# A first norm moved ahead of its constants, a busy TensorE at entry, and five contraction-outermost groups in the first tile of an eight-core encoder kernel

## The chip, the cores and the metric

The kernel runs on all 8 cores of one Trainium2 chip. Each core computes one batch row of 4096 frames, and the cores do not communicate. The metric is the device time of the slowest core, in microseconds (us). The cores view of a profile counts cores 0 to 3 as die 0 and cores 4 to 7 as die 1.

Executions of this program come in two states: with the kernel before, five runs from 4569.86 to 4578.76 us and one of 5423.23 us. In the slow state the cores of one die, sometimes of both, show a lower granted TensorE clock and run some per cent longer (in the slow runs of the changed kernel 4763.0 to 5355.1 us at 0.838 to 0.949; the cores of its fast runs took 4558.4 to 4573.2 us at 0.995 to 0.998). Fast runs are compared with fast runs here. Where a profile fell into the slow state on one die, only its other die is read, and it is compared with the same die of the other kernel.

## The reference, cut to what matters

```python
for l in range(2):                                   # DEPTH
    h = rmsnorm(x, norm1_g[l])                       # x: (8, 4096, 1024) float32
    proj = einsum('bsd,de->bse', h, w_in[l])         # q,k,v,r,fz,B,C,x_in,g_A,g_B
    log_a = log_sigmoid(fz @ w_fg2[l] + b_fg[l]) / 16.0      # the forget gate
    o = gla_chunk_causal(q * 128**-0.5, k, v, log_a)         # chunks of 64 frames
    y_a = (headnorm(o) * gla_norm_g[l] * silu(r)) @ w_oa[l]
    y_b = (B * causal_conv3(C * x_in)) @ w_ob[l]
    x = x + (sigmoid(g_A) * y_a + sigmoid(g_B) * y_b) @ w_o[l]
    h2 = rmsnorm(x, norm2_g[l])
    x = x + (silu(h2 @ w_gate[l]) * (h2 @ w_up[l])) @ w_down[l]
return rmsnorm(x, final_g)
```

## The kernel before

A core does four phases (mixer, FFN, mixer, FFN), each over 8 tiles of 512 frames. The weights of a phase are streamed again for every tile, in blocks of mostly 1024 KB (bf16) through four slots of on-chip memory. The weights arrive in fp32. In the first tile of the first mixer the load itself casts them to bf16, and even blocks are stored to a bf16 scratch. The odd blocks are cast and stored in the second tile. From the third tile on, loads come from the scratch.

```python
if s == 0 or (s == 1 and bi % 2):                    # issue_loads: the cast loads
    dma("pool", [], [("ws", sl)], fsem[sl], ... in_=wblock(k, l, bi))
else:
    dma("sp", [("scr", k, l, bi)], [("ws", sl)], wsem[sl], ... in_=scr[(k, l, bi)])
...
if s == bi % 2 and steps[s][0] == 0:                 # get_block: store to the scratch
    dma("sp", [("ws", sl)], [("scr", k, l, bi)], stsem[sl], ...)
```

The kernel has eight banks of PSUM, `pb[0]` to `pb[7]`, and `bank()` gives them out in a ring, in program order. A mixer tile starts with the section below. With the ring reset at the tile's start, `fza` takes bank 0, q0 and q1 take 1 and 2, the gate's four products take 3 to 6, q2 and q3 take 7 and 0, and the four groups of the first v block take 1 to 4.

```python
def gate1():
    bs = [bank() for _ in range(4)]
    mms(...)                                         # four products of fza with wfg
    for hh in range(4):
        op("act", ... func=AF.Exp, scale=-1.0, ...)  # "the gate's first Exp" when hh == 0
        op("act", ... func=AF.Ln, bias=1.0)
...
sl, wk, w = get_block("fzq")
b = bank()
fm_group(b, w, wk, 0, h_, hk)                        # 8 matmuls
op("dve", [BK(b)], ["fza", BK(b)], ...tensor_copy(out=fza, in_=pb[b][:, :]))
for hh in range(4):
    if hh == 2:
        gate1()
    b = bank()
    fm_group(b, w, wk, 128 + hh * 128, h_, hk)
    op("act", [BK(b)], [("qT", hh), BK(b)], ...activation(out=qT[:, hh, :], in_=pb[b]...))
...
def v_half(hf, after):                               # v0 here, k, then v1
    sl, wk, w = get_block("v%d" % hf)
    for ts in range(NTS):
        b = bank()
        tm_group(b, w, wk, ts, h_, hk)
```

The entry of the program, before the first tile:

```python
load_x(0, "act")
issue_loads(1)
for n, t, src in (("cst", ...), ("pk", ...), ("wfg", ...)):
    dma("act", ...)
op("dve", ["cst"], ["ident16"], ...)                 # VectorE waits here for a DMA
...
op("dve", ["pk"], ["nbfg"], ...)
op("dve", [], ["ones32"], ...memset(ones32[:], 1.0 / D))
...                                                  # Pool waits for x, then:
issue_loads()
set_ring(list(range(8)))
norm_first()                                         # squares, sums on TensorE with ones32, h
```

## Time and profile before

The three timed runs took 4575.52, 4576.48 and 4578.76 us.

| what | number |
|---|---|
| TensorE busy, slowest core (1) | 99% of 4574.1 us |
| first Square on ScalarE | 9.31 us |
| first sum of squares on TensorE | 22.78 us |
| first h | 34.04 us |
| gate's first Exp, tiles one / two / three, mean of 8 cores | 44.3 / 215.2 / 387.9 us |
| spacing of that Exp in later mixer tiles, at full clock | 164.65 us |

The gate's first Exp serves as a milestone below: "gate two" is its time in the second tile. These are lines of the page of the kernel before. The first two are the span and the busy time of each engine; the third is the queue of cast loads (packets, MB, share of the 16 DMA engines' span); the last is the chain of waits by engine.

```profile
span 4574.1 us, 63583 instructions; the slowest of 8 cores (4548.1 to 4574.1 us)
PE 4520.0 (99%) x21880; PEld 2046.2 (45%) x21880; DVE 2014.2 (44%) x3171; ACT 1551.2 (34%) x2996; POOL 190.1 (4%) x348
...
q0 software_dynamic: 7392, 92.80, 15.1%
...
PE 95%; DMA 4%; DVE 0%; issue 0%; ACT 0%; ACTq 0%; SPq 0%; DVEq 0%; POOLq 0%
```

The kernel is bound by TensorE, except where weights arrive too slowly. 92.80 MB (counted in bf16) in 15.1% of 4574.1 us is 7.8 us of all 16 engines for a 1024 KB cast block.

The timeline of core 1's entry follows. A line has start, busy time, engine, source line, what was done, and in brackets the idle time or start of a wait and what ended it.

```profile
9.31 1.15 ACT L408 ACTIVATE sb_sq<-sb_xT 128x512 f32<-128x512 f32 x2
...
22.03 0.23 DVE L814 CAST sb_ident<-sb_cst 128x128 bf16<-128x128 f32 x1 [22.03 <-DMA sb_cst<-cst]
...
22.36 0.17 DVE L821 MEMSET sb_ones<- 128x128 f32 x1
22.78 9.59 PE L329 MATMUL pb<-sb_sq,sb_ones 128*128 128x512 f32 x16 [22.78 <-DVE sb_ones L821]
...
34.04 5.39 DVE L420 SCALAR_TENSOR_TENSOR sb_hT<-sb_xT,sb_pk,sb_rstd 128x512 bf16<-128x512 f32 x8 [4.31 <-ACT sb_rstd L400]
...
47.88 7.66 PE L329 MATMUL pb<-sb_wsl,sb_hT 128*128 128x512 bf16 x32
```

ScalarE had a square ready near 10.5 us. VectorE stood behind a constant's DMA until 22.03 us, so the `ones` for TensorE's sums came at 22.36 and all the sums after it.

The windows of core 1 show where the DMA engines are full. The columns are the window and its length; busy time and count of PE, PEld, DVE, ACT, POOL; the granted clock; the DMA share; GB/s.

```profile
60.00:110.00 50.00, 50.00 (x267) 22.93 (x266) 24.22 (x44) 24.55 (x52) 6.04 (x12) 1.00 1.01 191
160.00:210.00 50.00, 47.07 (x224) 20.87 (x222) 24.38 (x37) 4.50 (x12) 3.58 (x7) 1.00 1.01 210
280.00:400.00 120.00, 119.76 (x601) 54.23 (x600) 68.93 (x112) 51.29 (x110) 8.78 (x17) 1.00 0.77 222
```

In the first two tiles the DMA share is 1.01; later it is 0.77. TensorE idles 2.9 us (50 less 47.07) at the end of tile one. The wait table of core 1 from 36 to 4500 us (who waits for whom: total us, times, longest us) begins with the weight loads, and no wait for a q copy is in it:

```profile
PE pb L329 <- DMA sb_wsl<-w_mix: 6.0, 4, 4.4
```

Next, the start of the fourth tile on core 1, from the timeline. L494 is the gate's Exp, L532 the copies of q out of PSUM, and the matmuls with `sb_hT` on the right of `sb_wsl` are the v groups.

```profile
555.10 0.69 ACT L494 ACTIVATE sb_arena<-pb,sb_nbfg 128x512 f32<-128x512 f32 x1
...
557.09 7.07 PE L329 MATMUL pb<-sb_wsl,sb_hT 128*128 128x512 bf16 x32
...
560.53 1.07 ACT L532 ACTIVATE sb_arena<-pb 128x512 bf16<-128x512 f32 x2
```

The third q copy, the first of the pair at 560.53, ends at 561.11, after the third v group has started (560.54). It costs nothing before the change, because that v group uses another bank.

Three windows of the fourth tile on core 1 show a stretch at 0.81 of the full clock. The clock records of the trace give this level as 0.8125, or 13/16; the only other levels that they hold, on any core, are 1 and 0.5.

```profile
560.00:565.00 5.00, 5.00 (x24) 2.19 (x22) 4.69 (x8) 3.23 (x6) 0.00 (x0) 0.96 0.94 299
565.00:570.00 5.00, 5.00 (x20) 2.07 (x19) 2.37 (x4) 1.86 (x4) 0.00 (x0) 0.81 0.98 311
570.00:575.00 5.00, 5.00 (x23) 2.24 (x22) 1.38 (x2) 0.60 (x1) 0.00 (x0) 0.93 0.67 243
```

Such a stretch is called a dip below. Its loss is its length times 0.1875, which is 1 less 0.8125.

### The profile page before, as it was taken

How to read it: one execution, taken by the hardware profiler on the slowest of the kernel's cores; microseconds unless marked ns; L12 is line 12 of the kernel's file. 1: busy time of each engine (PE TensorE's matmuls, PEld its weight loads, DVE VectorE, ACT ScalarE, POOL GpSimd, SP SyncE). 2: the span in 40 equal slices, each digit the busy share in tenths (PEclk: the TensorE clock that was granted, in tenths of full speed). 3: DMA queues.
4: the chain of work that ended last, by engine and by line, in shares of the span. 5: the costliest groups of instructions: out<-in, count | busy, mean ns of one | idle time of the engine just before them, and what ended most of it. 6: DMA issues, size and time to landing. Idle time of an engine off the chain costs nothing.

```text
span 4574.1 us, 63583 instructions; the slowest of 8 cores (4548.1 to 4574.1 us)
## 1 busy us (share of the span) xinstructions
PE 4520.0 (99%) x21880; PEld 2046.2 (45%) x21880; DVE 2014.2 (44%) x3171; ACT 1551.2 (34%) x2996; POOL 190.1 (4%) x348
## 2 busy tenths in 40 slices
PE   7999999999999999999999999999999999999998
PEld 3444444444444444444444444444444444444443
DVE  3554555565562222222245655554554523333332
ACT  3453453344341111111143453353453322222221
POOL 0100000000000000000000000000000000000000
PEclk9999999999999999999999999999999999999999
DMA  9988777668778676676656565555555555555552
GB/s 199 211 228 237 198 178 209 188 168 213 201 180 240 200 211 197 196 206 197 189 170 194 152 202 187 171 176 190 171 168 195 187 188 189 189 185 187 189 189 88
DMA packets 124488, 870.23 MB, mean 190 GB/s; under 512 B 14512, under 2 KB 14640, under 8 KB 48048
## 3 DMA queue, kind: packets, MB, share of 16 engines
q1 hardware_dynamic: 115776, 770.75, 49.9%
q0 software_dynamic: 7392, 92.80, 15.1%
q8 instruction: 183, 3.00, 0.3%
q10 hardware_dynamic: 1008, 2.62, 0.2%
q14 instruction: 129, 1.06, 0.1%
HBM read 868.48 MB, written 148.37 MB: 222 GB/s over the span
## 4 chain that ended last, share of the span: by engine, by line
PE 95%; DMA 4%; DVE 0%; issue 0%; ACT 0%; ACTq 0%; SPq 0%; DVEq 0%; POOLq 0%
PE pb L329 90%; PE pb L341 4%; DMA sb_wsl<-w_mix 1%; DMA sb_xT<-xs 1%; PE pb L626 1%; DMA sc_mix_v<-sb_wsl 1%; DMA sc_mix_o<-sb_wsl 0%; DMA sb_cst<-cst 0%; DMA sc_mix_ob<-sb_wsl 0%; PE pb L515 0%; DMA sc_mix_oa<-sb_wsl 0%; DMA sb_wsl<-sc_mix_k 0%; DVE sb_hT L420 0%; DVE sb_xT L800 0%; ACTq L363 0%
## 5 line engine op out<-in xcount | busy, mean ns | idle before, releaser
L329 PE MATMUL pb<-sb_hT,sb_wsl 128*128 128x512 bf16 x8768 | 1948.6, 382 | 3.1 <-DVE sb_hT L420 1.9
L329 PEld LDWEIGHTS pb<-sb_hT,sb_wsl 128*128 128x128 bf16 x8768 | 851.1, 98 | 1065.7 <-issue 110.4
L329 PE MATMUL pb<-sb_arena,sb_wsl 128*128 128x512 bf16 x3324 | 729.0, 379 | 2.3 <-DMA sb_wsl<-w_mix 1.2
L329 PE MATMUL pb<-sb_hT,sb_arena 128*128 128x512 bf16 x3136 | 685.6, 380 | 2.0 <-ACT sb_tmp L761 2.0
L766 DVE TENSOR_TENSOR sb_arena<-pb,sb_tmp 128x512 bf16<-128x512 f32 x352 | 243.3, 691 | 779.8 <-PE pb L329 644.1
L761 ACT ACTIVATE sb_tmp<-pb 128x512 f32<-128x512 f32 x352 | 209.9, 597 | 1097.9 <-PE pb L329 1062.1
L329 PEld LDWEIGHTS pb<-sb_arena,sb_wsl 128*128 128x128 bf16 x3324 | 324.9, 98 | 396.5 <-issue 5.9
L329 PEld LDWEIGHTS pb<-sb_hT,sb_arena 128*128 128x128 bf16 x3136 | 307.5, 98 | 377.9 <-issue 14.7
L329 PE MATMUL pb<-sb_wsl,sb_hT 128*128 128x512 bf16 x2048 | 458.3, 381 | 4.4 <-DMA sb_wsl<-w_mix 4.4
L456 DVE TENSOR_TENSOR sb_xT<-pb,sb_xT 128x512 f32<-128x512 f32 x256 | 171.3, 689 | 615.5 <-PE pb L329 538.2
L329 PE MATMUL pb<-sb_arena 128*128 128x512 bf16 (+1 forms) x2052 | 388.3, 354 | 0.0
L329 PEld LDWEIGHTS pb<-sb_wsl,sb_hT 128*128 128x128 bf16 x2048 | 197.5, 98 | 242.9 <-issue 15.2
L329 PEld LDWEIGHTS pb<-sb_arena 128*128 128x128 bf16 (+1 forms) x2052 | 165.7, 97 | 208.6 <-issue 27.0
L532 ACT ACTIVATE sb_arena<-pb 128x512 bf16<-128x512 f32 x64 | 36.2, 591 | 589.4 <-PE pb L329 589.4
L668 DVE SCALAR_TENSOR_TENSOR sb_tmp<-sb_ub,sb_pk,sb_tmp 128x512 f32<-128x512 f32 x256 | 192.1, 750 | 79.6 <-ACT sb_halo L662 65.7
L341 PE MATMUL pb<-sb_arena,sb_wsl 128*128 128x512 bf16 x1024 | 226.2, 379 | 0.8 <-DVE sb_tmp L710 0.8
L438 DVE SCALAR_TENSOR_TENSOR sb_hT<-sb_xT,sb_pk,sb_rstd 128x512 bf16<-128x512 f32 x248 | 173.9, 746 | 30.8 <-ACT sb_rstd L400 26.4
L378 ACT ACTIVATE sb_sq<-sb_xT 128x1024 f32<-128x1024 f32 x152 | 159.4, 1049 | 43.4 <-DMA sb_xT<-xs 23.9
L661 ACT ACTIVATE sb_tmp<-sb_ub,sb_pk 128x512 f32<-128x512 f32 x128 | 103.9, 811 | 199.3 <-DVE sb_ub L658 197.1
L675 ACT ACTIVATE sb_arena<-pb 128x512 bf16<-128x512 f32 x256 | 149.8, 591 | 59.0 <-PE pb L329 55.8
L632 ACT ACTIVATE sb_arena<-pb,sb_pk 128x256 bf16<-128x256 bf16 x256 | 120.6, 471 | 140.1 <-PE pb L626 128.2
L587 DVE SCALAR_TENSOR_TENSOR sb_S_1<-sb_S_0,sb_gam,pb 128x256 f32<-128x256 f32 x256 | 122.5, 478 | 98.8 <-PE pb L329 83.0
(95 smaller groups left out, 2746.1 us busy)
## 6 DMA issues: line engine op xcount, KB each, us to landing
sb_wsl<-sc_mix_cv SPq DMA_DIRECT2D x116, 1280.0 KB, 7.7
sb_arena<-sc_ffn_f SPq DMA_DIRECT2D x98, 1024.0 KB, 5.8
sb_wsl<-sc_ffn_f SPq DMA_DIRECT2D x78, 1024.0 KB, 5.9
sb_arena<-sc_ffn_d SPq DMA_DIRECT2D x70, 704.0 KB, 5.2
xs<-sb_xT SPq DMA_DIRECT2D x48, 1024.0 KB, 6.0
sb_xT<-xs SPq DMA_DIRECT2D x96, 512.0 KB, 10.2
sb_wsl<-sc_ffn_d SPq DMA_DIRECT2D x58, 704.0 KB, 5.5
sb_wsl<-sc_mix_ob SPq DMA_DIRECT2D x30, 1024.0 KB, 5.7
```

Source lines behind the costliest of these rows:

```text
L329: return lambda pe: pe.matmul(out, lhsT, rhs, start=first, stop=last)
L341: ins = e.h.matmul(pb[b][:, :], w[:, kc, col0:col0 + 128], rhsT[:, kc, :], start=(kc == 0), stop=(kc == KC - 1))
L378: lambda h, j=j, i=i: h.activation(out=sq[i][:], in_=xT[xb][:, 2 * j:2 * j + 2, :], func=AF.Square))
L438: lambda h, kc=kc: h.scalar_tensor_tensor(out=hT[xb][:, kc, :], in0=xT[xb][:, kc, :], scalar=pkc(g0 + kc), in1=rstd[:], op0=ALU.mult, op1= ...
L456: lambda h, b=b, dc=dc: h.tensor_tensor(out=xT[xb][:, dc, :], in0=pb[b][:, :], in1=xT[xb][:, dc, :], op=ALU.add))
L587: lambda h, c=c, h2=h2, hh=hh: h.scalar_tensor_tensor(out=S32[1 - c][:, hh, :], in0=S32[c][:, hh, :], scalar=gam[:, hh, 2 * ts + c:2 * ts ...
L632: lambda h, src=src, dst=dst, par=par: h.activation(out=dst, in_=src, func=AF.Copy, scale=pkc(96 + l * 2 + par)))
L661: lambda h, u=u, cc=cc, cw=cw, cacc=cacc: h.activation(out=cacc[:], in_=ub[u][:, 2:T + 2], func=AF.Identity, scale=cw(2), bias=pkc(80 + l ...
L668: lambda h, j=j: h.scalar_tensor_tensor(out=cacc[:], in0=ub[u][:, j:T + j], scalar=cw(j), in1=cacc[:], op0=ALU.mult, op1=ALU.add))
L675: lambda h, b=b, dst=dst, cc=cc: h.activation(out=dst[:, cc, :], in_=pb[b][:, :], func=AF.Sigmoid))
L761: lambda h, b=b, si=si: h.activation(out=tmp[si][:], in_=pb[b][:, :], func=AF.Silu))
L766: lambda h, b=b, si=si, fc=fc: h.tensor_tensor(out=hid[:, fc, :], in0=pb[b][:, :], in1=tmp[si][:], op=ALU.mult))
```

## The change

The intent is to start TensorE's work earlier. VectorE writes `ones` first and does its constants after the norm. TensorE multiplies `ones` with itself while it waits. The aim is that the sums do not begin at half speed, as they did in the profile before (0.85 us a pass at first, 0.43 later); that this work would prevent it was the author's estimate. In the first tile the five q-section groups (`fza` and q0 to q3) go through the contraction together: all five use the first piece of h, then the second, and so on, so that they can start when the first piece is there. The code that arranges this takes five banks at once, and it does so in every tile. Cuts are marked with `...`.

```diff
         def norm_first():
-            b = bank()
+            b, b2 = bank(), bank()
+            def busy(n):
+                mms([BK(b2)], [(mm(pb[b2][:, 0:128], ones32[:, :], ones32[:, :], True, True), ["ones32"]) for _ in range(n)])
+            busy(40)
             for j in range(4):
 ...
                 for c in range(2):
                     mms(... sums of squares ...)
+                if j < 3:
+                    busy(6)
             tk.record([], [BK(b)], (tk.E["pe"].sem, tk.E["pe"].cnt, "pe"))
             rstd_of(b)
-            b = bank()
-            mms([BK(b)], [... for _ in range(12)])
+            busy(12)
 ...
             sl, wk, w = get_block("fzq")
-            b = bank()
-            fm_group(b, w, wk, 0, h_, hk)
-            op("dve", [BK(b)], ["fza", BK(b)], ...)
+            bs = [bank() for _ in range(5)]
+            if s == 0:
+                fm_groups_kco([(bs[i], w, wk, i * 128) for i in range(5)], h_, hk)
+            else:
+                fm_group(bs[0], w, wk, 0, h_, hk)
+            op("dve", [BK(bs[0])], ["fza", BK(bs[0])], ...)
             yield
             for hh in range(4):
                 if hh == 2:
                     gate1()
-                b = bank()
-                fm_group(b, w, wk, 128 + hh * 128, h_, hk)
+                b = bs[1 + hh]
+                if s:
+                    fm_group(b, w, wk, 128 + hh * 128, h_, hk)
                 op("act", [BK(b)], [("qT", hh), BK(b)], ...)
 ...
         issue_loads(1)
-        for n, t, src in (("cst", cst[:], cst_d), ("pk", pk[:], pk_d), ("wfg", wfg[:], wfg_d)):
-            dma("act", ...)
-        op("dve", ["cst"], ["ident16"], ...)
 ...
+        op("dve", [], ["ones32"], lambda h: h.memset(ones32[:], 1.0 / D))
 ...
-        op("dve", ["pk"], ["nbfg"], ...)
-        op("dve", [], ["ones32"], lambda h: h.memset(ones32[:], 1.0 / D))
+        for n, t, src in (("pk", pk[:], pk_d), ("wfg", wfg[:], wfg_d), ("cst", cst[:], cst_d)):
+            dma("act", ...)
 ...
         norm_first()
+        op("dve", ["pk"], ["nbfg"], ...)
+        op("dve", ["cst"], ["ident16"], ...)
```

With the change the q section takes banks 0 to 4 in every tile, the gate 5, 6, 7 and 0. The v groups still take 1 to 4, so the third v group must now wait until ScalarE has copied the third q group out of bank 3.

More of the change, by code (lines that the diff above doesn't have):

```diff
@@ L412, in norm_first @@
                     mms([BK(b)] if j + c == 0 else [], [(mm(pb[b][:, :], ones32[:, :], sq[i][:, c, :], j + c == 0, j + c == 4), ["ones32", ("sqh", i, c)])])
+                if j < 3:
+                    busy(6)
             tk.record([], [BK(b)], (tk.E["pe"].sem, tk.E["pe"].cnt, "pe"))
             rstd_of(b)
-            b = bank()
-            mms([BK(b)], [(mm(pb[b][:, 0:128], ones32[:, :], ones32[:, :], True, True), ["ones32"]) for _ in range(12)])
+            busy(12)
             for kc in range(KC):
@@ L521, in mixer @@
             sl, wk, w = get_block("fzq")
-            b = bank()
-            fm_group(b, w, wk, 0, h_, hk)
-            op("dve", [BK(b)], ["fza", BK(b)], lambda h, b=b: h.tensor_copy(out=fza, in_=pb[b][:, :]))
+            bs = [bank() for _ in range(5)]
[3 more added lines that the diff above has]
+                fm_group(bs[0], w, wk, 0, h_, hk)
+            op("dve", [BK(bs[0])], ["fza", BK(bs[0])], lambda h: h.tensor_copy(out=fza, in_=pb[bs[0]][:, :]))
             yield
@@ L809, in build_nc @@
         issue_loads(1)
-        for n, t, src in (("cst", cst[:], cst_d), ("pk", pk[:], pk_d),
-                          ("wfg", wfg[:], wfg_d)):
-            dma("act", [], [n], tk.newsem("c_" + n), lambda q, t=t, src=src: q.dma_start(out=t, in_=src))
-        op("dve", ["cst"], ["ident16"], lambda h: h.tensor_copy(out=ident16[:], in_=cst[:, 0:128]))
         epsb = sb("epsb", [128, 1], F32)
         lnp = sb("lnp", [128, 1], F32)
+        mhalf = sb("mhalf", [128, 4], F32)
+        op("dve", [], ["ones32"], lambda h: h.memset(ones32[:], 1.0 / D))
         op("dve", [], ["epsb"], lambda h: h.memset(epsb[:], EPS))
-        mhalf = sb("mhalf", [128, 4], F32)
         op("dve", [], ["mhalf"], lambda h: h.memset(mhalf[:], -0.5))
-        op("dve", ["pk"], ["nbfg"], lambda h: h.tensor_scalar_mul(out=nbfg[:], in0=pk[:, 108:116], scalar1=-1.0))
-        op("dve", [], ["ones32"], lambda h: h.memset(ones32[:], 1.0 / D))
+        for n, t, src in (("pk", pk[:], pk_d), ("wfg", wfg[:], wfg_d), ("cst", cst[:], cst_d)):
+            dma("act", [], [n], tk.newsem("c_" + n), lambda q, t=t, src=src: q.dma_start(out=t, in_=src))
         for q in xsem[0]:
@@ L826, in build_nc @@
         norm_first()
+        op("dve", ["pk"], ["nbfg"], lambda h: h.tensor_scalar_mul(out=nbfg[:], in0=pk[:, 108:116], scalar1=-1.0))
+        op("dve", ["cst"], ["ident16"], lambda h: h.tensor_copy(out=ident16[:], in_=cst[:, 0:128]))
         casts = {}
```

## The prediction

> **What bounds the kernel.** TensorE: the page gives it 99% busy, the chain of waits is 95% TensorE. From the third tile on a tile takes 165.4 us (spacing of the gate's first Exp in the timeline) and TensorE has no gaps (its waits after 400 us: 10 us in all, nearly all in the last norm). Two stretches differ. (1) Entry, slowest core: the first Square runs at 9.3 us, but VectorE's queue stands behind the constants (cast at 22.03 us, ones at 22.36), so all eight sums of squares run from 22.8 to 32.4, the first half at half speed (0.85 us a pass, later 0.43); Ln, Exp, then h from 34.04; the first matmul group is paced by h (0.66 us each) to 39.6. (2) Tiles one and two: in the windows the DMA share is 0.97 to 1.03 from 10 to 280 us. By the queue table the cast loads cost 92.8 MB in 15.1% of 16 engines' span, 7.8 us a 1024 KB block, 9.8 a 1280 KB one; with half the blocks stored, plus x, about 205 us of DMA time for tile one, against 168 us of TensorE work. TensorE starts with the loads 8 to 9 us ahead (landed 38.2, 45.7, 54.3; used 47.9, 54.8, 62.7), and at the tile's end waits for them (201 us; again 252 and 273).
>
> **What the change does at entry.** x still lands last at 21.1 us (third quarter 20.0). The squares start near 9 us; the 40 constant products (0.24 us each warm, double cold) keep TensorE going until about x's second half. After it: 2 sums, 6 fillers, 2 sums, about 5 us; Ln and Exp 1.4. First h at about 27 (before 34.0), first real matmul 28.4 (35.05), 40 matmuls at 0.216 end near 37 (the five groups and the gate ended at 48.9; now about 38.4). So TensorE is 8 to 10 us earlier at the first v block. [...]
>
> **What is left of it.** Loads after x are issued at 21.6 as before and DMA is saturated [...]. So TensorE meets the landings: waits at the conv blocks near 80 us and on, and the second tile starts nearly when it did (213.8 for its gate). I keep 1 to 2 us.
>
> **A cost in every later tile.** Five banks are now taken at once also for later tiles: third and fourth q groups move from banks 7, 0 to 3, 4; the third and fourth v groups use 3, 4 as before. Those q copies on ScalarE stand behind the gate's table load and eight Exp and Ln. In the timeline the third q copy ends 0.57 us AFTER the third v group starts, in every tile from the second on, on both cores read (395.90 against 395.34). Before, another bank hid it. Now TensorE waits 0.57 plus about 0.17 us for the release (read at the h pacing): 0.73 us in each of 14 TensorE-bound tiles, 10 us. In tile one the same wait is about 3 us, hidden by the loads.
>
> **Sum.** 4576.5 - 1.5 + 10.2 = 4585 us; range 4577 to 4589. Faster by over 2%: 0.003; within 2%: 0.99; slower: 0.007.
>
> **Shown right by:** first h near 27; TensorE waits on weight DMA growing by about 5 us before 280 us; gate of tile two within 3 us of 213.8; a new TensorE wait on ScalarE's q copy, 0.7 us, some 14 times; tile spacing 166.1 in place of 165.4.
>
> **Wrong if:** earlier issue makes loads land earlier, so up to 8 us stay (about 4578); the bank wait is hidden; or clock dips, about 1 us each, move.

The sum came to 4576.5 - 1.5 + 10.2 = 4585.2 us. That the constant products would keep the sums of x's second half at full speed is the author's estimate. Its figures are from the profile before: 24 passes on constants took 2.84 us from 32.21 us on, so a product of two passes took 0.24 us, and "double" is the ratio of the 0.85 and 0.43 us of the sums. The wait for DMA rests on the windows before, with a DMA share of 0.97 to 1.03 from 10 to 260 us.

## More of the kernel before

Experiments ran on several chips ("chip 6", "chip 14" and so on), and each has runs of the kernel before on that chip beside it.

Last, the granted clock. The cores view of the kernel before:

```profile
core 1: 4574.1 us, clock 0.993
...
die 0 (median of its cores): 4571.1 us, clock 0.993
die 1 (median of its cores): 4557.3 us, clock 0.997
```

Die 0 is 14 us slower than die 1, at a clock 0.004 lower.

Counting the trace's clock records, cores 0 to 3 had 21 or 22 dips each, worth 20.9 to 22.2 us; 14 or 15 of them began 7 to 14 us after a tile's gate. Cores 4 to 7 had none or one.

## The result and the profile after

The one fast run of the changed kernel among its six timed runs took 4573.28 us (two further executions, beside these six, were fast too: 4574.36 and 4572.33 us); the five fast runs of the kernel before took 4569.86 to 4578.76 us. Five runs of the changed kernel and one of the kernel before were in the slow state and are left aside. A ratio here is the mean time of one kernel's fast runs over that of the other's of the same rounds, so it is not quite the ratio of the medians quoted. The ratio of fast runs is 0.9995, with a 95% interval from 0.9977 to 1.0013: the same. The predicted class was right, but the predicted cost of 8.5 us did not appear, and 4573 lies below the range.

The profile of the changed kernel fell into the slow state on die 1, as its cores view shows:

```profile
core 1: 4567.5 us, clock 0.995
...
die 0 (median of its cores): 4570.4 us, clock 0.995
die 1 (median of its cores): 5315.0 us, clock 0.842
```

Die 0 is undisturbed and is compared with die 0 of before. This is core 1's entry after the change:

```profile
1.16 0.17 DVE L823 MEMSET sb_ones<- 128x128 f32 x1 [1.16 <-PEq L154]
1.48 10.67 PE L329 MATMUL pb<-sb_ones 128*128 128x128 f32 x80 [1.48 <-DVE sb_mhalf L825]
...
20.55 2.64 PE L329 MATMUL pb<-sb_sq,sb_ones 128*128 128x512 f32 x4 [2.29 <-ACT sb_sq L413]
...
28.96 5.39 DVE L425 SCALAR_TENSOR_TENSOR sb_hT<-sb_xT,sb_pk,sb_rstd 128x512 bf16<-128x512 f32 x8 [7.37 <-ACT sb_rstd L400]
29.99 8.79 PE L341 MATMUL pb<-sb_hT,sb_wsl 128*128 128x512 bf16 x40
...
40.21 3.61 PE L329 MATMUL pb<-sb_wsl,sb_hT 128*128 128x512 bf16 x16
...
46.44 3.61 PE L329 MATMUL pb<-sb_wsl,sb_hT 128*128 128x512 bf16 x16 [2.62 <-ACT sb_arena L541]
```

The first h comes 5.1 us earlier (28.96 against 34.04), and the first v group 7.7 us earlier (40.21 against 47.88). The third v group then waits 2.62 us for ScalarE's q copy (L541). By the second tile the lead is nearly gone: gate two moves from 216.3 to 214.9 us on core 1, and it is 1.3 to 2.4 us later on the three other cores of die 0.

These two windows of core 1 answer to those of before:

```profile
60.00:110.00 50.00, 47.03 (x250) 21.11 (x249) 24.37 (x43) 24.80 (x54) 6.01 (x12) 1.00 1.01 194
160.00:210.00 50.00, 48.57 (x229) 21.80 (x228) 25.05 (x38) 4.34 (x12) 3.58 (x7) 0.98 1.01 223
```

The DMA share is 1.01 as before, and TensorE now idles 3.0 us between 60 and 110 us, where it idled not at all. The longer of its two stops there ends like this:

```profile
81.84 0.32 SPq L299 DMA_DIRECT2D sc_mix_cv<-sb_wsl  x1
82.02 2.32 PE L329 MATMUL pb<-sb_hT,sb_wsl 128*128 128x512 bf16 x10 [1.74 <-DVE sb_arena L580]
```

The first line is the store of a conv block to the scratch, which is issued when the block has landed: at 81.78 us by the trace's semaphore record, against 80.97 before. The next conv block landed at 102.57 us, against 102.47 before. So the loads are no earlier, but TensorE is: before, it came to the first of these blocks only at 85.55. The view names VectorE for this wait and ScalarE for the other (1.16 us), but both stopped matmuls are the first of a block and start 0.24 to 0.25 us after its landing, as the one at 251.30 does, for which the table names a DMA. An earlier issue did not help either: the first block of r weights was issued at 39.33 us instead of 48.58 but landed at 65.40 instead of 62.65. The last block of tile one landed at 200.05 instead of 201.30.

The start of the fourth tile on core 1 shows the predicted bank wait:

```profile
554.89 0.69 ACT L499 ACTIVATE sb_arena<-pb,sb_nbfg 128x512 f32<-128x512 f32 x1
...
556.88 3.62 PE L329 MATMUL pb<-sb_wsl,sb_hT 128*128 128x512 bf16 x16
...
560.33 1.07 ACT L541 ACTIVATE sb_arena<-pb 128x512 bf16<-128x512 f32 x2
561.05 3.18 PE L329 MATMUL pb<-sb_wsl,sb_hT 128*128 128x512 bf16 x14 [0.55 <-ACT sb_arena L541]
```

Counted from the gate's first Exp, the third v group starts 0.72 us later than before (6.16 us after it, against 5.44); 0.55 us of this is shown as idle time. The wait table of core 1, from 30 us on, counts the wait 16 times, the first of them (2.6 us) in tile one:

```profile
PE pb L329 <- ACT sb_arena L541: 11.1, 16, 2.6
PE pb L329 <- DMA sb_wsl<-w_mix: 6.0, 3, 4.3
```

At full clock a tile is now 165.36 us long, 0.71 us more than the 164.65 of before. The same three windows of that tile, though, have lost their dip:

```profile
560.00:565.00 5.00, 4.45 (x22) 1.86 (x21) 4.06 (x7) 3.03 (x6) 0.00 (x0) 1.00 1.01 366
565.00:570.00 5.00, 5.00 (x25) 2.29 (x24) 2.85 (x5) 1.87 (x4) 0.00 (x0) 1.00 0.99 338
570.00:575.00 5.00, 5.00 (x27) 2.29 (x25) 1.38 (x2) 0.60 (x1) 0.00 (x0) 1.00 0.54 168
```

On die 0, no dip begins near a gate any more; 9 or 10 a core remain elsewhere in the program. The means over cores 0 to 3 add up as follows:

| die 0, mean of 4 cores | before | after | difference |
|---|---|---|---|
| start to gate three | 387.4 us | 389.0 us | +1.6 |
| gate three to end | 4183.0 us | 4181.2 us | -1.8 |
| of it: 14 bank waits of 0.71 us | | | +9.9 |
| of it: lost in dips after gate three | 18.37 us | 6.46 us | -11.9 |

The last two rows sum to -2.0 us, against -1.8 measured. So the wait was there in the predicted size, and fewer dips paid for it. This is one profile of each kernel; that the bank order and not chance took the dips away is tested below.

### The profile page after: what moved, and what is told of

Same layout as the page of the kernel before. It is cut to its first block, busy times and chain, and to the rows that moved or that the text cites. A ratio compares the mean times of both kernels' runs of the same rounds, so it can differ in the third digit from the quotient of the medians.

```text
span 5327.9 us, 63749 instructions; the slowest of 8 cores (4567.5 to 5327.9 us)
## 1 busy us (share of the span) xinstructions
PE 5292.3 (99%) x21996; PEld 2239.1 (42%) x21996; DVE 2023.3 (38%) x3171; ACT 1561.7 (29%) x2996; POOL 187.5 (4%) x348
## 3 DMA queue, kind: packets, MB, share of 16 engines
q1 hardware_dynamic: 115776, 770.75, 41.8%
q10 hardware_dynamic: 1008, 2.62, 0.2%
## 4 chain that ended last, share of the span: by engine, by line
PE 95%; DMA 4%; ACT 0%; issue 0%; DVE 0%; ACTq 0%; POOL 0%; POOLq 0%; SPq 0%; DVEq 0%
PE pb L329 89%; PE pb L341 5%; DMA sb_wsl<-w_mix 2%; DMA sc_mix_cv<-sb_wsl 1%; PE pb L635 1%; DMA sc_mix_k<-sb_wsl 0%; DMA sb_xT<-x 0%; DMA sc_mix_o<-sb_wsl 0%; DMA sc_mix_ob<-sb_wsl 0%; PE pb L520 0%; DMA sb_wsl<-sc_mix_k 0%; ACT sb_arena L499 0%; ACT sb_arena L502 0%; DVE sb_xT L809 0%; ACT L499 0%
## 5 line engine op out<-in xcount | busy, mean ns | idle before, releaser
L329 PE MATMUL pb<-sb_hT,sb_wsl 128*128 128x512 bf16 x8728 | 2239.9, 424 | 5.3 <-DMA sb_wsl<-w_mix 4.7
L329 PEld LDWEIGHTS pb<-sb_hT,sb_wsl 128*128 128x128 bf16 x8728 | 915.6, 106 | 1292.0 <-issue 1075.7
L329 PE MATMUL pb<-sb_arena,sb_wsl 128*128 128x512 bf16 x3324 | 854.9, 425 | 0.2 <-DMA sb_wsl<-w_mix 0.2
L329 PE MATMUL pb<-sb_hT,sb_arena 128*128 128x512 bf16 x3136 | 829.7, 436 | 0.0
L770 ACT ACTIVATE sb_tmp<-pb 128x512 f32<-128x512 f32 x352 | 210.2, 597 | 1432.0 <-PE pb L329 1386.6
L329 PEld LDWEIGHTS pb<-sb_arena,sb_wsl 128*128 128x128 bf16 x3324 | 354.5, 107 | 489.9 <-issue 414.6
L329 PEld LDWEIGHTS pb<-sb_hT,sb_arena 128*128 128x128 bf16 x3136 | 341.1, 109 | 486.4 <-issue 486.4
L329 PE MATMUL pb<-sb_wsl,sb_hT 128*128 128x512 bf16 x2048 | 524.1, 419 | 10.1 <-DMA sb_wsl<-w_mix 5.1
L329 PE MATMUL pb<-sb_arena 128*128 128x512 bf16 (+1 forms) x2052 | 463.0, 401 | 0.0
L329 PEld LDWEIGHTS pb<-sb_arena 128*128 128x128 bf16 (+1 forms) x2052 | 182.2, 105 | 265.7 <-issue 263.8
L341 PE MATMUL pb<-sb_arena,sb_wsl 128*128 128x512 bf16 x1024 | 259.4, 418 | 0.6 <-DMA sb_wsl<-w_mix 0.6
L541 ACT ACTIVATE sb_arena<-pb 128x512 bf16<-128x512 f32 x64 | 36.1, 591 | 674.4 <-PE pb L329 665.0
L667 DVE TENSOR_TENSOR sb_ub<-pb,sb_tmp 128x512 f32<-128x512 f32 x128 | 88.5, 691 | 242.0 <-PE pb L329 230.3
L341 PEld LDWEIGHTS pb<-sb_arena,sb_wsl 128*128 128x128 bf16 x1024 | 107.2, 105 | 142.2 <-issue 105.9
```

Source lines behind the costliest of these rows:

```text
L329: return lambda pe: pe.matmul(out, lhsT, rhs, start=first, stop=last)
L341: ins = e.h.matmul(pb[b][:, :], w[:, kc, col0:col0 + 128], rhsT[:, kc, :], start=(kc == 0), stop=(kc == KC - 1))
L667: lambda h, b=b, u=u, csb=csb: h.tensor_tensor(out=ub[u][:, 2:T + 2], in0=pb[b][:, :], in1=csb[:], op=ALU.mult))
L770: lambda h, b=b, si=si: h.activation(out=tmp[si][:], in_=pb[b][:, :], func=AF.Silu))
```

## The experiments

There were 18 runs. Three questions were asked: does the bank change alone make both the wait and the missing dips; is the entry's gain lost to the DMA engines; and is the short pause of TensorE itself what removes the dips? The theory was "yes" to each. The rivals were chance or a property of the chip for the dips, and, for the entry, a gain taken by the bank wait of tile one.

### Parts of the change, on chip 6

`e1_banks_only` is the kernel before with the five banks taken at once, in the order of computation of before.

```diff
             sl, wk, w = get_block("fzq")
-            b = bank()
-            fm_group(b, w, wk, 0, h_, hk)
+            bs = [bank() for _ in range(5)]
+            fm_group(bs[0], w, wk, 0, h_, hk)
 ...
-                b = bank()
+                b = bs[1 + hh]
```

> The kernel before, with only the five banks of the q section taken at once in every tile. Theory (loads absorb the entry's gain; the bank wait costs 0.7 us a tile; its pause also removes the 13/16 clock dips that stand in the same place, 1.1 us each): a wait of TensorE on the q copy about 15 times, 0.7 us each; undipped cores 165.36 us a tile in place of 164.65; on a die that dipped before, the dips 8 to 13 us after the gate gone, so the slowest core is within 3 us of before. Rival (the entry's gain of 8 to 10 us reaches the end and pays for the bank wait; the dips come and go by chance): 10 us slower than before, and dips where they were.

`e2_banks_back` is the changed kernel with five banks at once in the first tile only, the order of before in the others.

```diff
-            bs = [bank() for _ in range(5)]
+            bs = [bank() for _ in range(5 if s == 0 else 1)]
 ...
-                b = bs[1 + hh]
+                b = bs[1 + hh] if s == 0 else bank()
```

> The changed kernel with the old order of banks in every tile but the first. Theory: no wait on the q copy after tile one, undipped cores back at 164.65 us a tile, the dips after the gate back on the die that has them, the whole within 3 us of before. Rival: about 10 us faster than before and than the changed kernel, 4564 to 4567 us.

`e3_entry_only` is the changed kernel with the whole q section of before, in every tile: only the norm and the constants are changed.

```diff
-            bs = [bank() for _ in range(5)]
-            if s == 0:
-                fm_groups_kco([(bs[i], w, wk, i * 128) for i in range(5)], h_, hk)
-            else:
-                fm_group(bs[0], w, wk, 0, h_, hk)
+            b = bank()
+            fm_group(b, w, wk, 0, h_, hk)
 ...
-                b = bs[1 + hh]
-                if s:
-                    fm_group(b, w, wk, 128 + hh * 128, h_, hk)
+                b = bank()
+                fm_group(b, w, wk, 128 + hh * 128, h_, hk)
```

> The constants and the fillers of the entry alone, no contraction outermost, banks as before. Theory: first h near 29 us in place of 34, and the gate of the second tile within 2 us of before (213 to 217 us), whole within 2 us of before. Rival: gate of the second tile and the end 5 us earlier.

`e4_changed_again` is the changed kernel, unedited.

> The changed kernel once more, for a profile with both dies undisturbed. Theory: undipped cores 165.36 us a tile, gate of the second tile 213 to 217 us, few dips after the gate; whole within 3 us of before.

On this chip the kernel before ran at 4603.5 to 4630.8 us (median 4616.0 of 11 runs), slower than on the chip of the first result. Its dips are longer, 15.1 us each in e3's profile, and hit die 1 (the kernel before was not traced on this chip). A die that dips enough is over 1% longer than the other, so some of these runs are labelled slow; the ratios use only those labelled fast. `e1` gave 0.9949 [0.9899, 0.9998], `e4` 0.9946 [0.9894, 0.9998], `e2` 0.9997 [0.9894, 1.0100]; `e3` got no interval, and its fast runs took 4618.65 and 4613.81 us. Within the 2% class all are the same. `e1` and `e4` were expected within 3 us of before and came out about 24 us faster by these ratios: dips cost more on this chip than on the first, from which the expectation was made.

The reason is plainer core by core. The next table takes all runs of this chip, slow ones too, and picks cores instead of runs: in the middle column the cores whose mean granted clock was at least 0.996, and at the right cores 4 to 7 wherever their clock was above 0.97, which leaves out the slow state. In brackets is the number of cores averaged.

| chip 6 | cores at full clock | cores 4 to 7, dipping |
|---|---|---|
| before | 4553.3 us (40) | 4604.4 us (44) |
| e3: entry only | 4554.1 (25) | 4597.9 (28) |
| e2: all but the banks of later tiles | 4553.2 (11) | 4596.1 (32) |
| e1: banks only | 4564.0 (24) | 4579.9 (16) |
| e4: the change | 4564.7 (29) | 4580.2 (24) |

At full clock the banks cost 10.7 us (e1) and the entry is worth nothing (e3 and e2 within 1 us of before). On cores 4 to 7 the banks alone gain 24.5 us. The slowest core is a dipping one, so the time follows the right column. Single runs scatter: the means of these four cores in a run reach from 4568 to 4605 us with the new bank order (e1 and e4) and from 4576 to 4611 us with the old one (before, e2, e3), but six of the ten runs with the new order lie below all 26 with the old. Two fast-state profiles show it. First a line of the cores view and three windows of e3, core 4:

```profile
core 4: 4617.5 us, clock 0.982
```

```profile
565.00:570.00 5.00, 5.00 (x21) 2.13 (x20) 3.21 (x5) 1.86 (x4) 0.00 (x0) 0.84 0.97 279
570.00:575.00 5.00, 5.00 (x20) 2.07 (x19) 2.02 (x3) 0.00 (x0) 0.00 (x0) 0.81 0.95 334
575.00:580.00 5.00, 5.00 (x26) 2.38 (x25) 0.75 (x2) 1.59 (x2) 0.00 (x0) 0.81 0.67 248
```

Then the same of e4, core 4:

```profile
core 4: 4587.8 us, clock 0.991
```

```profile
560.00:565.00 5.00, 4.46 (x22) 1.86 (x21) 3.27 (x5) 4.71 (x9) 0.00 (x0) 1.00 0.82 299
565.00:570.00 5.00, 5.00 (x25) 2.28 (x24) 4.07 (x7) 2.47 (x6) 0.00 (x0) 1.00 1.00 336
570.00:575.00 5.00, 5.00 (x25) 2.29 (x24) 2.00 (x3) 0.06 (x1) 0.00 (x0) 1.00 0.70 206
```

In the clock records of these profiles, cores 4 and 5 of e3 had 26 dips each (73.7 us lost), 15 of them near a gate. In e4, cores 4 to 7 had 10 each (28.4 us lost), none near a gate. In e1, cores 4 and 5 had 9 each (25.5 us lost) and one near a gate. The profile of e2 was slow on die 0; on its other die, 13 to 15 dips a core began near a gate. So the dips near the gate go with the bank order: they are there in before (on the first chip), e2 and e3, and all but gone in e1 and e4. The difference in dips from e3 to e4 (-45.3 us) and the waits (+10) would make core 4 faster by 35 us; it is faster by 29.7, and the rest was not traced.

The traces of e1 to e4 that are kept are of other executions, with other core times. What remains of the first profiles agrees in size with the counts: the views above, and the mean clock of core 4 (0.982 in e3, 0.991 in e4). In the kept traces, e1, e2 and e3 have at most two dips a core and none near a gate, and e4 has a few long stretches, so they say nothing for or against the link. They do confirm the price of the bank order at full clock: 164.66 us a tile in e2 and e3, 165.36 in e1 and e4.

### The pause alone, and a later entry, on chip 14

`e5_pause_only` keeps the banks and the entry of before but makes the third v group wait for the third q copy, which is the wait that the bank order causes.

```diff
-                    tm_group(b, w, wk, ts, h_, hk)
+                    tm_group(b, w, wk, ts, h_, (lambda kc: hk(kc) + [("qT", 2)]) if (ts, hf) == (2, 0) else hk)
```

> The kernel before with its own banks, but the third v group of each tile made to wait for the third q copy, which it does not need. If the pause of TensorE is what removes the clock dips: a wait of 0.7 us in each tile from the second on, undipped cores 165.36 us a tile, no dips 8 to 14 us after the gate, and a time within 0.3% of the kernel with the banks alone (0.995 of before on a chip that dips much, 1.00 on one that dips little). If it is the change of banks and not the pause: 165.36 us a tile and the dips still there, 10 us slower than before.

`e6_pause_short` does the same with an earlier event, the gate's last Ln, for a shorter pause.

```diff
-                    tm_group(b, w, wk, ts, h_, hk)
+                    tm_group(b, w, wk, ts, h_, (lambda kc: hk(kc) + [("spb", 3)]) if (ts, hf) == (2, 0) else hk)
```

> The same, but waiting for the gate's last Ln, which ends 0.08 us after the group would start: a pause of about 0.25 us. If any break in the dense stretch does: 164.9 us a tile on undipped cores, no dips after the gate, 7 us less than with the long pause. If the break must be long: the dips stay, and the time is before's plus 3 us.

`e7_late` is the changed kernel with 40 more constant products ahead of the first h's matmuls.

```diff
-            busy(12)
+            busy(52)
```

> The changed kernel with 52 in place of 12 fillers after the norm, so that the first real matmul comes 9.5 us later (39.5 us in place of 30). If the loads of tile one absorb the entry's gain: gate of the second tile at most 3 us later than in the changed kernel (213 to 221 us). If the gain reaches the end: 9.5 us later (223 to 227 us).

The kernel before ran at full clock on this chip, on all 60 cores of its undisturbed dies (a mean granted clock of 0.996 or more leaves no room for the dips of chip 6, where 73.7 us of 4617.5 were lost, 0.016 of the clock), and its fast runs took 4559.27 to 4563.51 us. So the question about the pause could not be answered here. What was measured is the price. Averaged over full-clock cores, before takes 4556.0 us, e5 4566.6 (+10.6), e6 4560.1 (+4.1). The tile spacing grew by 0.71 us in e5 and by 0.22 us in e6. The ratios are 1.0024 [0.9995, 1.0054] and 1.0024 [0.9984, 1.0064]. A fast run of e5 at 4599.94 us had a long stretch of low clock on each core of die 1 (261 us from 28 us on for cores 4 and 5, 106 to 124 us from 4461 us on for cores 6 and 7). None of them began near a gate.

In e7 the gate of tile one came at 48.6 us on average over the cores, against 39.9 in e4, yet gate two came at 218.4 us, against 216.2. The products that made it late stand in the timeline of core 1:

```profile
28.12 11.77 PE L329 MATMUL pb<-sb_ones 128*128 128x128 f32 x104
39.73 2.54 PE L341 MATMUL pb<-sb_hT,sb_wsl 128*128 128x512 bf16 x11
```

An entry 8.7 us later than in e4 made gate two only 2.2 us later. Tile one, from gate to gate, took 169.8 us instead of 176.3: most of the delay was absorbed, as it is if the loads set the tile's end.

### DMA relieved in tile one, and stores spread out, on chip 4

`e8_before_nostore` and `e9_changed_nostore` are the kernel before and the changed kernel with no stores in tile one: all blocks are cast again in tile two and stored then.

```diff
-                if s == 0 or (s == 1 and bi % 2):
+                if s == 0 or s == 1:
 ...
-            if s == bi % 2 and steps[s][0] == 0:
+            if s == 1 and steps[s][0] == 0:
```

> The kernel before, with all stores of bf16 weight blocks moved from the first tile to the second (about 35 us of DMA time less in tile one, more in tile two). Serves as the base of the next run. If loads bound tile one: the gate of the second tile a few us earlier than in before (208 to 213 us), TensorE without waits on weights in tile one; the third tile later.

(The 35 us are an estimate. On the profile page of before, the queue that carries the stores (q1) moved 770.75 MB in 49.9% of the span, 3.1 us of all 16 engines for 1024 KB, and the ten blocks stored in tile one hold 11520 KB.)

> The changed kernel with the same move. If the first tile's DMA load is what absorbed the entry's gain, the gate of the second tile now comes 5 to 8 us earlier than in the run before it (202 to 207 us). If something else absorbs it: no more than 2 us earlier.

All three runs of e8 were slow. In e9 the TensorE of core 4 waits for no DMA at all in tile one. The first line of its wait table from 36 to 212 us (the only other is 0.2 us for VectorE), and a window with the DMA share at 0.79:

```profile
PE pb L329 <- ACT sb_arena L541: 2.8, 1, 2.8
```

```profile
110.00:160.00 50.00, 50.00 (x266) 22.88 (x265) 34.22 (x57) 33.06 (x73) 8.24 (x13) 1.00 0.79 129
```

`e10_spread` is e2 with the stores spread over the first four tiles by a fixed list, and the casts of the next phase begun one tile later (the last edit is not shown).

```diff
+        STORE_AT = [0, 1, 2, 3, 1, 0, 2, 1, 0, 3, 2, 1, 0, 2, 3, 0, 1, 2, 0, 3]
 ...
-                if s == 0 or (s == 1 and bi % 2):
+                if p_of(s) == 0 and s <= STORE_AT[bi]:
 ...
-            if s == bi % 2 and steps[s][0] == 0:
+            if steps[s][0] == 0 and s == STORE_AT[bi]:
```

> The changed kernel with the old banks after tile one and the stores spread over tiles one to four (6, 5, 5, 4 blocks), the first casts of the next weights one tile later. If the loads of tiles one and two cost about 15 us beyond TensorE's work and hid the entry's gain of 8 us: the gate of the third tile 10 to 20 us earlier than before's 388, and the whole 10 to 20 us under before on cores without dips; dips as before's.

`e11_spread_short` is e10 with the short pause of e6.

> The same with the short pause (third v group waits for the gate's last Ln). If the short pause removes the dips after the gate as the long one did: no dips 8 to 14 us after the gate on dies that show them in the run before it, and faster than it there; on dies without dips 0.22 us a tile slower, 3 us in all. If it is too short: dips in both runs alike.

In e10 gate two came at 206.1 us, about 9 us earlier than before, but gate three at 391.2, later than before (387.9). The wait table of core 5 from 30 to 400 us says where it went:

```profile
PE pb L332 <- DMA sb_wsl<-sc_mix_r: 15.0, 1, 15.0
```

One block of tile two was issued at 212.49 us and landed at 252.10. The gain of tile one was given back in one wait of tile two. Fast runs took 4577.62 and 4585.17 us against 4562.27 to 4565.74 for before. All runs of e11 were disturbed (lowest 4617.91), so it decides nothing.

### Another spread, the pauses again, on chip 12

`e12_spread2` has e10's edits with another list: it stores the first six blocks in tile one and the others one to three tiles later, and fetches the next tile's x later in the first two tiles. The casts of the next phase begin as in e10.

```diff
+        STORE_AT = [0, 0, 0, 0, 0, 0, 1, 2, 3, 1, 2, 3, 1, 2, 3, 1, 2, 3, 1, 2]
 ...
-                side += [lead(8), pre(), lead(8 if kind == "ffn" else 34), norm_h(s + 1)]
+                side += [lead(26 if s < 2 else 8), pre(), lead(8 if kind == "ffn" else 16 if s < 2 else 34), norm_h(s + 1)]
```

> The changed kernel with old banks after tile one, the six blocks that a tile needs first stored in tile one (so tile two starts on short loads), the other 14 in tiles two to four, and x of tiles two and three fetched 18 groups later. If the e10 kernel's wait at the start of the second tile (12 to 16 us on the second r block, loads of 25 to 40 us) came from casts, x and stores piled up there: that wait under 4 us, gate of the third tile at 370 to 380 us (before 388), and on cores without dips 10 to 18 us under before. If the loads cannot be evened out: gate of the third tile at 385 or later, no gain.

`e13_pause_again` is e5 and `e14_short_again` is e6, unedited, tried on another chip. `e15_before_nostore` repeats e8.

> The pause without the change of banks once more, for a chip whose kernel before shows dips (the first try fell on one without). If the pause removes the dips: none 8 to 14 us after the gate, faster than before by 0.7 us a tile less than the dips' loss. If the banks did it: the dips there, 10 us slower than before. On a chip without dips: 10 us slower either way.

> The 0.25 us pause once more. Dips after the gate gone if any break will do; still there if the break must be longer. Without dips on the chip: 3 us slower than before.

> The kernel before with the stores of tile one moved to tile two, once more, for a profile in the fast state: the base of the changed kernel with the same move, whose second gate came at 210 us. If loads absorbed the entry's gain: gate of the second tile 4 to 6 us later than there (214 to 217), the first tile 165 to 166.5 us long from gate to gate in both, in place of 171 and 176 with the stores.

The kernel before again ran at full clock, on all 48 cores of its undisturbed dies (4554.6 us on average). e13 took 4564.1 us on such cores (+9.5), e14 4557.3 (+2.7; ratio 1.0007 [0.9978, 1.0036]), e12 4558.6 (+4.0; ratio 1.0017 [0.9988, 1.0046]). No spread of the stores made the program faster. e12 missed its expected gate three of 370 to 380 us: in its profile, which was slow on die 1, the four cores of die 0 reached it at 381.6 to 394.7 us. By the wait table of core 0, no wait for a DMA before 400 us was longer than 1.7 us; what held gate three back was not traced.

Chip 12 is not quite free of dips near the gate. One run of before had die 0 at a clock of 0.985, as on chip 6, and was not traced. In e12, which has the old bank order after tile one, cores 2 and 3 had five dips near the gates of later tiles; in e13 and e14, with the pauses, no core had one in a later tile. But e15, without a pause, had only one such dip on each of four cores, so these profiles don't decide it.

e15 completes the test of the entry. In both no-store kernels tile one is bound by TensorE (165.9 us from gate to gate in e15, 165.6 in e9), and core 4's waits in tile one of e15 hold no DMA either:

```profile
PE pb L329 <- DVE sb_hT L420: 1.3, 5, 0.3
```

| mean of 8 cores | gate one | gate two | gate three |
|---|---|---|---|
| before (first chip) | 44.3 us | 215.2 us | 387.9 us |
| the change, e4 (chip 6) | 39.9 | 216.2 | 388.9 |
| e15: before, no stores in tile one (chip 12) | 49.5 | 215.3 | 427.6 |
| e9: the change, no stores in tile one (chip 4) | 44.7 | 210.2 | 426.6 |

(The e4 row is from its first profile; die 0 of the profile after gives 39.6, 215.8 and 389.0 us.)

Without stores in tile one, the change's lead is 4.8 us at gate one and 5.1 us at gate two: it passes through, although e9 has the wait for the q copy in tile one too (2.8 us). With them, 4.4 us at gate one becomes -1.0 at gate two. Both no-store kernels then pay over 45 us in tile two, where all blocks are cast again, and there the lead shrinks to 1.0 us: DMA is the bound there too (core 4 of e9 waits 43 us for weights between 212 and 430 us). (Gate one is about 5 us later in both no-store kernels than in the kernels with stores, so e9 is compared with e15, not with before.) The two ran on different chips and there is one profile of each; no core of either lost more than 3 us to dips in the whole run.

### A last try of the pause, on chip 4 again

`e16_before_look` is the kernel before, `e17_pause_third` is e5 and `e18_short_third` is e6, all unedited.

> The kernel before, for its profile on this chip: tells whether the chip shows dips 8 to 14 us after the gate (as the first chip and chip 6 did) or none (chips 14, 4, 12), and so what the two runs after it can tell.

> Pause of 0.7 us, old banks. If the profile of the run before it shows dips after the gate: none here if the pause removes them, the same number if the banks did. Without dips there: 165.36 us a tile and 10 us slower.

> Pause of 0.25 us, old banks. With dips on this chip: gone if any break will do, there if it must be longer. Without: 164.88 us a tile and 3 us slower.

e16 ran at full clock (4559.22 us), and its trace has no dip on any core. Its gates came at 44.1, 214.4 and 387.6 us, and its later mixer tiles are 164.65 us long on all cores. On full-clock cores before takes 4552.7 us, e17 4562.3 (+9.6) and e18 4557.1 (+4.4; ratio 1.0039 [0.9991, 1.0088]). Before, e17 and e18 each also had runs in which two or four cores were some 30 to 50 us longer at a clock of 0.984 to 0.991, with the pause and without it; where it was traced (e17, e18), it was one stretch of 161 us on a pair of cores, not a row of dips. So no try of the pause alone met a kernel before that was seen to dip at the gate on the same chip: the traces of e16 show none here, and on chips 14 and 12 the kernel before was not traced.

## Why the prediction was right and wrong

**The entry came earlier: right, less than predicted.** The first h was predicted near 27 us and came at 28.96 us; the five groups were predicted to end near 37 us and ended at 38.78 (29.99 plus 8.79). TensorE idled 2.29 us before the sums of x's second half, and the clock records show a stretch at half clock of 3.4 us at 22 us, so part of those sums ran at half speed in spite of the constant products (2.64 us for four passes, which take 0.43 us each at full clock). What sets off such a stretch was not shown.

**The lead is absorbed: right.** Gate two was predicted within 3 us of 213.8; on die 0 it came at 214.9 to 216.7 us, from 1.4 us earlier to 2.4 us later than before on the same core. Not even the 1.5 us of the sum were left: the mean is 1.0 us later. On core 1 the steps can be followed: the first v group is 7.7 us earlier, 2.6 us of it go to the wait for the q copy, 3.2 us to longer waits for loads in tile one (6.1 in place of 2.9, counted by landings as above), and gate two is 1.4 us earlier. At full clock e2 and e3 gain nothing. The cause was tested from both sides: an entry 8.7 us later costs 2.2 us (e7), and the lead passes through tile one only where DMA is relieved there (e9 against e15). The rival, that the bank wait of tile one takes the gain, fails: e9 has this wait and keeps its lead. The trace shows it on one block too: at a DMA share of 1.01, the first block of r weights, issued 9.25 us earlier, landed 2.75 us later.

**TensorE's DMA waits grow by 5 us: right in kind, too large.** By the wait tables the mean of die 0 rose from 7.3 to about 10 us. If the waits are added that end 0.22 to 0.27 us after a landing and stand under another engine's name, it rose from 8.1 to 11.3 us (up to 285 us): about 3 us in either count. The conv blocks near 80 us, where the prediction put the first waits, are among them. The 2.6 us for the q copy in tile one came on top, hidden as predicted.

**The bank wait in each later tile: right.** Predicted were 0.73 us in 14 tiles, 10.2 us in all. The tile grew by 0.71 us, and the banks alone cost 10.7 us on full-clock cores (e1). The tile lengths I gave, 165.4 and 166.1, had dips of the slowest die mixed in; at full clock they are 164.65 and 165.36.

**The sum: wrong.** The step that failed reads "4576.5 - 1.5 + 10.2 = 4585 us". It holds the clock of the slowest core constant. At a constant clock the sum is nearly right: the change costs 11.4 us on full-clock cores of chip 6 (predicted: -1.5 + 10.2 = 8.7). But 4576.5 was the time of a die with 21 or 22 dips, and the change removed those near the gate: 11.9 us on die 0 after gate three. This term was named only as a risk ("clock dips, about 1 us each, move") and left out of the sum. The cores view of before, with die 0 14 us slower than die 1, had shown that the slowest core was a dipping one.

What the runs show is that the bank order of every later tile, not the entry, goes with the missing dips (e1 and e4 against e2 and e3 on chip 6). What they leave open:

- Whether the short stop of TensorE removes them, or something else in the bank order. Three tries of the stop alone fell on chips on which the kernel before was not seen to have such dips.
- Whether a stop of 0.22 us would be enough; it costs 2.7 to 4.4 us at full clock.
- What the dips are, and why one chip has them and another not. No run tested that.
- Why the slow state came as often as it did. It is the same level, 0.81, held: core 4 of the profile after stayed at it from 53 us on for 4396 us.

No version tried beats both kernels on cores at full clock. There, before, e2 and e3 are equal and fastest (chip 6). Where cores dip, the change and e1 are fastest, by about 0.5%.

## What to carry to other kernels

Before predicting by addition, read the clock of the core that sets the time: if its die runs some 10 us behind the other at a slightly lower clock, a change that rearranges TensorE's work can give or take that much, and the same edit can cost 11 us on cores at full clock and gain 25 us on cores that dip (both on chip 6). The earlier start was worth nothing here ahead of a tile with a DMA share of 1.01 (e3 and e2 within 1 us of before at full clock); check such a gain with an edit that makes the start later, and one that relieves the stretch. A helper that takes several buffers at once "for the first tile" changes the ring in every tile: write down which buffer each user gets, before and after, and who empties it.

## The granted clock, as these runs show it

- In the fast runs, with all eight cores busy, the mean granted clock of a core was 0.981 to 0.999. Dips lasted 5.1 to 5.6 us on average on the first chip's die 0 and 15.1 us each on cores 4 and 5 of e3's first profile, and they ended while TensorE stayed busy (5.00 of 5.00 us from 570 us on in before, at a mean clock of 0.93 in place of 0.81). Apart from stretches of 106 to 261 us in a fast run of e5 and one of 161 us in e17 and e18, only the slow state held the level (0.842 on average on die 1 of the profile after).
- Pairs of cores dipped alike within a die. In before, cores 0 and 1 lost 22.2 us each to dips, cores 2 and 3 20.9 us each. In e3's first profile, cores 4 and 5 had a mean clock of 0.982, core 6 0.995 and core 7 0.997; in e12, cores 2 and 3 had 10 dips each (mean clock 0.990 and 0.991), cores 0 and 1 had 4 (0.992).
- It differed between chips and with the order of work. The kernel before had 21 or 22 dips a core on one die of one chip and none at all in a profile on another (e16, all cores at 0.997 or 0.998); with another order of PSUM banks, which stops TensorE for 0.7 us a tile, the 14 or 15 near the gate were gone.
